# A 64-byte shift of the y buffers, a third seven-product piece in two blocks, and later loads of x and final_g, in a one-core gated short-convolution layer

## The chip, the cores and the metric

The kernel runs on one core of one Trainium2 chip. The metric is the device time of one execution in microseconds; the reported time is the median of several executions. One further execution is taken by the hardware profiler: the profile and its trace describe that execution.

## What is computed

`DEPTH` is 1, so the reference is one layer: an RMS norm of `x`, a modulation by `c` (adaLN), a gated short convolution, a gated residual, and a second RMS norm. D is 2048, E is 4096, the sequence has T = 256 tokens, all in float32.

```python
h = rmsnorm(x, norm_g)
mod = silu(c) @ ada_w + ada_b                  # shift, scale, gate: 3 x 2048
h = h * (1 + scale) + shift
b_gate, c_gate, v, g = split(h @ w_in, 4)      # w_in is 2048 x 16384
u = causal_depthwise_conv(c_gate * v, conv_w)  # width 3
y = b_gate * u * silu(g)                       # 256 x 4096
x = x + gate * (y @ w_out)                     # w_out is 4096 x 2048
return rmsnorm(x, final_g)
```

## The kernel before

**Precision.** Every large product is made of three products of a shorter float type: a float32 tile is split into `hi` (a rounding copy on ScalarE, `split_hi`, L315) and `lo` (the remainder, a subtraction on VectorE, `split_lo`, L320), and hi·hi, hi·lo and lo·hi are summed in PSUM.

**Input projection (L445).** The weights `w_in` are loaded tile by tile, split, and stand still in the array (`hi`, `lo`, 128x128 each); the tokens `hT` (hi and lo part of the modulated h, 16 tiles of 128 features) stream past, 256 columns per matmul. The first half of the columns is written to `mm_s` in an order planned by `plan()`, beside the sums that make shift and scale; the second half is written to `mm_b` by the loop over `ct` at L592. The results of a pair of 128 columns are gated, convolved and multiplied to y, and `split_y` (L396) stores hi and lo of y in a tile `ys[pair]`: 16 tiles of 128 x 2 x 2 x 256.

**Output projection (L753).** It runs over four blocks `dc` of 512 output columns. In a block, eight pieces `ep` of 512 rows of `w_out` are loaded by SyncE (`raw_o`, L771, 1 MB each), split, and multiplied with y. Here y stands still in the array and the split weights stream. A plain piece (`out_mm`, L640) has 2 token halves x 4 row tiles x 3 = 24 matmuls of 512 columns (L648, L649, L650). In the first three blocks the pieces in `SEVEN = (5, 6)` go another way (`seven`, L670): two 2x2 block products made with seven instead of eight block products (Winograd's form), 2 x 7 x 3 = 42 matmuls of 256 columns (L661). For these VectorE also forms sums of blocks of the weights (`sums_o`, L679, L685, L686), and the raw piece and the sums are each split (L684 and L687; L315 and L320). The matching sums of y are made once, in `token_forms` (L577, VectorE L583 to L586 and L590, ScalarE L589), into tiles `form`. `gather` (L715) adds the partial results at the end of a block on VectorE (L720), and `gated` (L791) multiplies by the gate, adds x, squares, and multiplies by `final_g` (L800 to L803). In the fourth block all eight pieces are plain, and each is first multiplied by the gate on VectorE (L778). The order of the pieces is `mix = (0, 1, 5, 2, 3, 6, 4, 7)`, in the fourth block 0 to 7.

**Buffers.** `hi`, the pieces loaded for the output projection and the splits each rotate over three buffers: tag `hi` holds the hi parts, tag `lo` holds `raw_o` and `sums_o`, tag `raw` holds the lo parts (and the first piece). A load waits until VectorE has read the tile that stood in its buffer. The stage's PSUM banks come in three pairs: one for `mm_o`, one for `mm_7`, one for the next block.

**Order.** A scheduler places each engine's instructions; SyncE issues nearly all loads in one queue, in order. x and `final_g` are loaded a second time for the end of the layer (L634, L635), into the tile `big`, which takes the space of `hT` and so waits for the last matmul of L445.

**Places in memory.** Pads named `line` to `line4` set where the buffers begin. In the built program the starts, counted in bytes past a multiple of 128 in each partition, are:

| buffer | used as | before | after |
|---|---|---|---|
| `hi`, `lo` in the input projection | stands still, L445 | 64 | 64 |
| `hT` | streams, L445 | 0 | 0 |
| `y`, `form` | stands still, L648 to L661 | 64 | 0 |
| `hi`, and `lo` in tag `raw` | streams, L648 to L661 | 64 | 64 |

All matmul operands begin at multiples of 256 bytes past these starts.

Of the kernel before, what the change touches and what calls it, by code (L numbers as in the profile page):

```python
# [31 lines left out]
ASLOT = 1024  # L32
# [85 lines left out]
def short_conv_layer(ctx: ExitStack, tc: tile.TileContext, x, c, norm_g, ada_w, ada_b, w_in, conv_w, w_out, final_g, out):  # L118
    nc = tc.nc
# [4 lines left out]
    line = ctx.enter_context(tc.tile_pool(name="line", bufs=1, side="right"))  # L124
    line.tile([P, 56], F32, tag="line", name="line")
    const = ctx.enter_context(tc.tile_pool(name="const", bufs=1))
    const.tile([P, 16], F32, tag="line0", name="line0")
    adap = ctx.enter_context(tc.tile_pool(name="adap", bufs=2))
    wpool = ctx.enter_context(tc.tile_pool(name="wpool", bufs=2))
    psum = ctx.enter_context(tc.tile_pool(name="psum", bufs=3, space=PSUM))  # L130
    hpool = ctx.enter_context(tc.tile_pool(name="hpool", bufs=1, side="right"))
    line2 = ctx.enter_context(tc.tile_pool(name="line2", bufs=1, side="right"))
    line2.tile([P, 48], F32, tag="line2", name="line2")
    slots = ctx.enter_context(tc.tile_pool(name="slots", bufs=NSLOT, side="right"))

    def slot(shape, name, dtype=F32):
# [157 lines left out]
    def modulate(k0, nk, sums):  # L294

        ks = slice(k0, k0 + nk)
        sums = sums.rearrange("p (s k) -> p s k", s=2)
        nc.vector.tensor_tensor(out=mod[:, :, ks], in0=sums, in1=bias[:, :, ks], op=ALU.add)
        for k in range(k0, k0 + nk):
            hf = xs[k // CT][:, k % CT, :]  # L300
            nc.scalar.activation(hh_[:, k], hf, AF.Identity, bias=mod[:, 0, k : k + 1], scale=mod[:, 1, k : k + 1])  # L301
# [3 lines left out]
            nc.vector.tensor_tensor(out=hl_[:, k], in0=hf, in1=hh_[:, k].bitcast(F32), op=ALU.subtract)  # L305

    def hi_tile():
        return wpool.tile([P, SLOT], F32R, tag="hi", name="hi", bufs=3)
# [132 lines left out]
    def product(dst, hi, lo, k, i, begins, left, ends):  # L441

        w, h = ((hi, hh_), (hi, hl_), (lo, hh_))[i]

        mm = last_mm[0] = nc.tensor.matmul(dst, w, h[:, k], start=begins and left, stop=ends, skip_group_check=True)  # L445
# [125 lines left out]

    KP = 8
    EP = 4
    SEVEN = (5, 6)
    forms = {}

    def token_forms(pair, u):  # L577

        sums = zs[0][:, 0].rearrange("p a (b f) -> p (a b) f", f=P)
        a11, a12 = u[:, 0, 0:P], u[:, 1, 0:P]  # L580
        a21, a22 = u[:, 0, P:T], u[:, 1, P:T]
        s1n, s2, s3, s4 = (sums[:, j] for j in range(4))
        nc.vector.scalar_tensor_tensor(out=s1n, in0=a21, scalar=-1.0, in1=a22, op0=ALU.mult, op1=ALU.subtract)  # L583
        nc.vector.scalar_tensor_tensor(out=s2, in0=s1n, scalar=-1.0, in1=a11, op0=ALU.mult, op1=ALU.subtract)
        nc.vector.tensor_tensor(out=s3, in0=a11, in1=a21, op=ALU.subtract)
        nc.vector.tensor_tensor(out=s4, in0=a12, in1=s2, op=ALU.subtract)  # L586
        form = adap.tile([P, ASLOT], F32R, tag="at", name="form", bufs=4)
        form = forms[pair] = form.rearrange("p (h s f) -> p h s f", h=2, f=P)
        nc.scalar.copy(form[:, 0], sums)  # L589
        nc.vector.tensor_tensor(out=form[:, 1], in0=sums, in1=form[:, 0].bitcast(F32), op=ALU.subtract)  # L590

    for ct in range(NS, NCT, 2):  # L592
        for q in QUARTERS:
# [34 lines left out]
        gate_piece()  # L628


    big = hpool.tile([P, 4, D], F32, tag="big", name="big")
    fg = big[:, 2, :]
    for t in range(TT):
        nc.sync.dma_start(big[:, t, :], x[t * P : (t + 1) * P, :])  # L634
    nc.sync.dma_start(fg, final_g.rearrange("(o d) -> o d", o=1).partition_broadcast(P))  # L635
    fsq = const.tile([P, TT, 4], F32, tag="fsq", name="fsq")
    LATE = 3
    NB = 256
# [31 lines left out]
    def seven(po, ps, ep, raw):  # L670
# [20 lines left out]
            return [ys[pair][:, k, h, t * P : (t + 1) * P] for h in range(2)]  # L691

        def f(pair, j):
            return [forms[pair][:, h, j] for h in range(2)]

        left, right = slice(0, NB), slice(NB, 2 * NB)
        for r in range(2):
# [17 lines left out]
    def gather(po, ps):  # L715


        res = big[:, 3, 0 : 2 * TT * NB].rearrange("p (t f) -> p t f", t=TT)
        u = big[:, 3, 2 * TT * NB :].rearrange("p (j f) -> p j f", f=NB)
        add = lambda out, a, b: nc.vector.tensor_tensor(out=out, in0=a, in1=b, op=ALU.add)  # L720
# [9 lines left out]
        return res  # L730

    part_sum = const.tile([P, TT], F32, tag="part_sum", name="part_sum")

# [14 lines left out]
            nc.sync.dma_start(out[t * P : (t + 1) * P, dd], r)  # L748

    n_ep = NCT // EP  # L750
    mix = (0, 1, 5, 2, 3, 6, 4, 7)
    orders = [mix, mix, mix, range(n_ep)]
    for dc in range(4):  # L753
        dcs = slice(dc * 512, (dc + 1) * 512)

# [11 lines left out]
        for ep in orders[dc]:  # L767

            first = dc == 0 and ep == 0
            raw = wpool.tile([P, SLOT], F32, tag="raw" if first else "lo", name="raw_o", bufs=3)  # L770
            nc.sync.dma_start(  # L771
                raw.rearrange("p (k f) -> p k f", k=EP),
                w_out[0, ep * EP * P : (ep + 1) * EP * P, dcs].rearrange("(k p) f -> p k f", p=P),
            )
            if dc == 3:

                raw3 = raw.rearrange("p (k f) -> p k f", k=EP)
                nc.vector.tensor_tensor(  # L778
                    out=raw3, in0=raw3, in1=gate(dc).unsqueeze(1).to_broadcast([P, EP, 512]), op=ALU.mult
                )  # L780
            if dc < 3 and ep in SEVEN:
                seven(po, ps, ep, raw)
                continue
            hi, lo = split(raw, SLOT, "raw")
            out_mm(po[0], 0, ep, hi, lo)
            if dc == 3 and ep >= n_ep - LATE:
                late.append((ep, hi, lo))
            else:
                out_mm(po[1], 1, ep, hi, lo)

        def gated(t, bank, c0, n):  # L791

            cs = slice(dc * 512 + c0, dc * 512 + c0 + n)
            r = big[:, t, cs]
            p0 = t * 512 + c0
            pr = big[:, 3, p0 : p0 + n]
            if dc == 3:
                nc.scalar.activation(pr, bank, AF.Square, scale=D**-0.5, accum_out=fsq[:, t, dc : dc + 1])
                return
# [7 lines left out]
                nc.vector.tensor_scalar_add(ps, ps, EPS)  # L807

        if dc < 3:
            res = gather(po, ps)  # L810
            po = [res[:, t] for t in range(TT)]
        gated(0, po[0], 0, 512)
        if dc == 3:
# [29 lines left out]
```

## Time and profile before

| what | value |
|---|---|
| median of 3 runs | 914.58 us (914.57 to 915.13) |
| the profiled execution | 915.32 us, of which 913.5 us are the span of its instructions |
| busy: PE, DVE, ACT | 894.8, 653.4, 476.4 us |
| first and last matmul of the output projection | start at 730.7 us and 903.5 us |
| matmuls of the output projection | 624 of 512 columns, 252 of 256 columns |

PE is TensorE's matmul row, DVE is VectorE, ACT is ScalarE, SPq is SyncE's queue. A row of a timeline begins with the start and the length in microseconds from the start of the span; `xN` joins N like instructions; in brackets stands the idle time of the engine before it and what ended it. A row of the groups ends with busy time, mean length in nanoseconds, and idle time before.

### The profile page before, as it was taken

How to read it: one execution, taken by the hardware profiler on the slowest of the kernel's cores; microseconds unless marked ns; L12 is line 12 of the kernel's file. 1: busy time of each engine (PE TensorE's matmuls, PEld its weight loads, DVE VectorE, ACT ScalarE, POOL GpSimd, SP SyncE). 2: the span in 40 equal slices, each digit the busy share in tenths (PEclk: the TensorE clock that was granted, in tenths of full speed). 3: DMA queues.
4: the chain of work that ended last, by engine and by line, in shares of the span. 5: the costliest groups of instructions: out<-in, count | busy, mean ns of one | idle time of the engine just before them, and what ended most of it. 6: DMA issues, size and time to landing. Idle time of an engine off the chain costs nothing.

```text
span 913.5 us, 16529 instructions
## 1 busy us (share of the span) xinstructions
PE 894.8 (98%) x7155; PEld 862.0 (94%) x7155; DVE 653.4 (72%) x655; ACT 476.4 (52%) x426; POOL 0.7 (0%) x6
## 2 busy tenths in 40 slices
PE   6999999999999999999999999999999999999995
PEld 4999999999999999999999999999999988888884
DVE  4889899989888886765545777555555567877992
ACT  6868856665558756743344434344433344444442
POOL 0000000000000000000000000000000000000000
PEclk9999999999999999999999999999999999999998
DMA  9999999999998686676666887556666476655642
GB/s 314 366 371 349 361 324 346 360 368 359 334 323 278 197 287 192 198 248 194 184 191 198 261 272 231 185 186 195 197 203 191 138 280 227 204 204 194 220 146 93
DMA packets 163753, 227.66 MB, mean 249 GB/s; under 512 B 5680, under 2 KB 104160, under 8 KB 163296
## 3 DMA queue, kind: packets, MB, share of 16 engines
q1 hardware_dynamic: 163552, 226.56, 75.0%
q8 instruction: 56, 0.92, 0.4%
q14 instruction: 17, 0.14, 0.0%
q10 hardware_dynamic: 128, 0.04, 0.0%
HBM read 224.49 MB, written 2.10 MB: 248 GB/s over the span
## 4 chain that ended last, share of the span: by engine, by line
PE 95%; DMA 3%; ACT 1%; DVE 0%; ACTq 0%; issue 0%; DVEq 0%
PE mm_s L445 38%; PE mm_b L445 38%; PE mm_o L649 4%; PE mm_o L650 4%; PE mm_o L648 4%; DMA raw_o<-in_sc_w_out_dram 2%; PE mm L661 2%; PE mm_o L661 1%; PE tp_idle L238 1%; DMA rows<-in_ada_b_dram 1%; PE mm_l L648 1%; PE mm_l L649 1%; PE mm_l L650 1%; PE sum L354 1%; ACT hi L315 0%; PE ps_gate L569 0%
## 5 line engine op out<-in xcount | busy, mean ns | idle before, releaser
L445 PE MATMUL mm_s<-hT,hi 128*128 128x256 f32 x2048 | 350.4, 277 | 0.1
L445 PE MATMUL mm_b<-hT,hi 128*128 128x256 f32 x2048 | 349.4, 276 | 0.0
L445 PEld LDWEIGHTS mm_s<-hT,hi 128*128 128x128 f32 x2048 | 308.2, 188 | 1.0 <-ACT hT L301 0.3
L445 PEld LDWEIGHTS mm_b<-hT,hi 128*128 128x128 f32 x2048 | 308.1, 188 | 0.5 <-issue 0.5
L445 PE MATMUL mm_b<-hT,lo 128*128 128x256 f32 x1024 | 282.6, 276 | 0.0
L445 PE MATMUL mm_s<-hT,lo 128*128 128x256 f32 x1024 | 282.2, 277 | 0.0
L320 DVE TENSOR_TENSOR lo<-raw,hi 128x2048 fp32r<-128x2048 f32 (+1 forms) x66 | 148.0, 2243 | 115.8 <-ACT hi L315 115.3
L315 ACT CAST hi<-raw 128x2048 fp32r<-128x2048 f32 (+1 forms) x66 | 123.7, 1874 | 195.1 <-PE mm_b L445 150.0
L445 PEld LDWEIGHTS mm_b<-hT,lo 128*128 128x128 f32 x1024 | 192.2, 188 | 0.5 <-issue 0.5
L445 PEld LDWEIGHTS mm_s<-hT,lo 128*128 128x128 f32 x1024 | 191.7, 188 | 0.3 <-DVE lo L320 0.2
L320 DVE TENSOR_TENSOR lo<-raw_s,hi 128x2048 fp32r<-128x2048 f32 (+1 forms) x80 | 147.5, 1849 | 36.6 <-ACT hi L315 35.6
L315 ACT CAST hi<-raw_s 128x2048 fp32r<-128x2048 f32 (+1 forms) x80 | 123.9, 1558 | 69.3 <-PE mm_s L445 58.9
L428 DVE SCALAR_TENSOR_TENSOR gv<-at,silu_c,gv 128x512 f32<-128x512 f32 x105 | 78.5, 749 | 2.5 <-DMA at<-in_ada_w_dram 0.8
L315 ACT CAST hi<-raw_o 128x2048 fp32r<-128x2048 f32 x26 | 49.6, 1907 | 58.1 <-DVE raw_o L778 24.0
L320 DVE TENSOR_TENSOR lo<-raw_o,hi 128x2048 fp32r<-128x2048 f32 x26 | 59.1, 2288 | 23.9 <-ACT hi L315 23.9
L466 ACT COPY acc<-mm_s 128x1024 f32<-128x1024 f32 x54 | 54.6, 1012 | 38.4 <-PE mm_s L445 38.4
L649 PE MATMUL mm_o<-lo,y 128*128 128x512 f32 x176 | 68.7, 390 | 0.8 <-DVE lo L320 0.8
L650 PE MATMUL mm_o<-hi,y 128*128 128x512 f32 x176 | 68.5, 389 | 0.0
L648 PE MATMUL mm_o<-hi,y 128*128 128x512 f32 x176 | 68.4, 390 | 0.0
L566 DVE SCALAR_TENSOR_TENSOR gacc<-at_g,silu_c,gacc 128x512 f32<-128x512 f32 x60 | 44.9, 748 | 6.2 <-DMA at_g<-in_ada_w_dram 5.2
L649 PEld LDWEIGHTS mm_o<-lo,y 128*128 128x128 f32 x176 | 33.1, 188 | 7.8 <-DVE lo L320 1.1
L650 PEld LDWEIGHTS mm_o<-hi,y 128*128 128x128 f32 x176 | 33.1, 188 | 6.7
(132 smaller groups left out, 584.4 us busy)
## 6 DMA issues: line engine op xcount, KB each, us to landing
raw<-in_sc_w_in_dram SPq DMA_DIRECT2D x64, 1024.0 KB, 5.6
raw_s<-in_sc_w_in_dram SPq DMA_DIRECT2D x47, 1024.0 KB, 7.5
raw_o<-in_sc_w_out_dram SPq DMA_DIRECT2D x32, 1024.0 KB, 5.2
at<-in_ada_w_dram SPq DMA_DIRECT2D x114, 256.0 KB, 7.8
raw_s<-in_sc_w_in_dram SPq DMA_DIRECT2D x33, 512.0 KB, 6.7
at_g<-in_ada_w_dram SPq DMA_DIRECT2D x32, 512.0 KB, 7.7
at<-in_ada_w_dram SPq DMA_DIRECT2D x6, 512.0 KB, 9.4
x<-in_x_dram SPq DMA_DIRECT2D x4, 512.0 KB, 6.1
```

The source lines that it names most:

```text
L238: nc.tensor.matmul(tp_idle, ident, ones[:, 0:1].to_broadcast([P, 512]), start=True, stop=True)
L315: nc.scalar.copy(hi[:, :n], raw[:, :n])
L320: nc.vector.tensor_tensor(out=lo[:, :n], in0=raw[:, :n], in1=hi[:, :n].bitcast(F32), op=ALU.subtract)
L354: nc.tensor.matmul(sums0[:, o * P : (o + 1) * P], rows[:, o // NK0, (o % NK0) * P : (o % NK0 + 1) * P], col.to_broadcast([P, P]), start=k ...
L428: nc.vector.scalar_tensor_tensor(out=gv, in0=at4[:, i], scalar=c_k, in1=gv, op0=ALU.mult, op1=ALU.add)
L445: mm = last_mm[0] = nc.tensor.matmul(dst, w, h[:, k], start=begins and left, stop=ends, skip_group_check=True)
L466: nc.scalar.copy(acc[ch, q], bank)
L566: nc.vector.scalar_tensor_tensor(out=ga, in0=at3[:, i, :], scalar=s, in1=ga, op0=ALU.mult, op1=ALU.add)
L648: nc.tensor.matmul(po, yh, hi[:, o], start=opens, stop=False, skip_group_check=True)
L649: nc.tensor.matmul(po, yh, lo[:, o], start=False, stop=False, skip_group_check=True)
L650: nc.tensor.matmul(po, yl, hi[:, o], start=False, stop=ct == NCT - 1, skip_group_check=True)
L661: mm = nc.tensor.matmul(dst, form[a], b, start=opens and i == 0 and bank not in first_of, stop=False, skip_group_check=True)
```

## The change

1. Pads: `line0` grows by 64 bytes, `line4` and `line2` shrink by 64 each. The tiles of `const`, `adap` (`form`, `at`, `gv`) and all slots (`y`, `z`, `gate`, `acc`, x) begin 64 bytes later; `hi`, `lo`, `raw` and `hT` stay.
2. `SEVEN` becomes `(5, 6, 7)`, used in the first two blocks; the third block keeps `(5, 6)`, the fourth stays plain. The sums of y for pairs 14 and 15 are made too. Their tiles find room in the two `gv` buffers and in a part `hT2` cut off from `hT` (its last two feature tiles, at the same address as before).
3. The order of the pieces becomes `(0, 1, 2, 5, 3, 6, 4, 7)`.
4. `big` has 3 rows of D, not 4; the scratch of `gather` and `gated` moves into the `z` tiles.
5. x and `final_g` are asked for inside the first block, behind the load of its fourth piece; in SyncE's queue of the built program they stand behind the fourth `raw_o` load of the block, where they stood behind the third.

```diff
-    const.tile([P, 16], F32, tag="line0", name="line0")
+    const.tile([P, 32], F32, tag="line0", name="line0")
...
-    line2.tile([P, 48], F32, tag="line2", name="line2")
+    line2.tile([P, 32], F32, tag="line2", name="line2")
...
-    wpool.tile([P, 32], F32, tag="line4", name="line4", bufs=1)
+    wpool.tile([P, 16], F32, tag="line4", name="line4", bufs=1)
...
-    hT = hpool.tile([P, KT, 2 * T], F32R, tag="big", name="hT")
-    hh_ = hT[:, :, 0:T]
-    hl_ = hT[:, :, T : 2 * T]
+    KB = KT - 2
+    hT = hpool.tile([P, KB, 2 * T], F32R, tag="big", name="hT")
+    hT2 = hpool.tile([P, KT - KB, 2 * T], F32R, tag="big2", name="hT2")
...
-    SEVEN = (5, 6)
+    SEVEN = (5, 6, 7)
...
-        form = adap.tile([P, ASLOT], F32R, tag="at", name="form", bufs=4)
-        form = forms[pair] = form.rearrange("p (h s f) -> p h s f", h=2, f=P)
-        nc.scalar.copy(form[:, 0], sums)
-        nc.vector.tensor_tensor(out=form[:, 1], in0=sums, in1=form[:, 0].bitcast(F32), op=ALU.subtract)
+        if pair < 14:
+            form = adap.tile([P, ASLOT], F32R, tag="at", name="form", bufs=4).rearrange("p (h s f) -> p h s f", h=2, f=P)
+            hi, lo = form[:, 0], form[:, 1]
+        elif pair == 14:
+            hi, lo = (adap.tile([P, 512], F32R, tag="gv", name="form_g").rearrange("p (s f) -> p s f", f=P) for _ in range(2))
+        else:
+            form = hpool.tile([P, 2, 4, P], F32R, tag="big2", name="form_h")
+            hi, lo = form[:, 0], form[:, 1]
+        forms[pair] = hi, lo
+        nc.scalar.copy(hi, sums)
+        nc.vector.tensor_tensor(out=lo, in0=sums, in1=hi.bitcast(F32), op=ALU.subtract)
...
-    big = hpool.tile([P, 4, D], F32, tag="big", name="big")
+    big = hpool.tile([P, 3, D], F32, tag="big", name="big")
+    res = zs[1].rearrange("p a b f -> p a (b f)")
     fg = big[:, 2, :]
-    for t in range(TT):
-        nc.sync.dma_start(big[:, t, :], x[t * P : (t + 1) * P, :])
-    nc.sync.dma_start(fg, final_g.rearrange("(o d) -> o d", o=1).partition_broadcast(P))
+
+    def load_ends(n):
+
+        if 0 <= n < TT:
+            nc.sync.dma_start(big[:, n, :], x[n * P : (n + 1) * P, :])
+        elif n == TT:
+            nc.sync.dma_start(fg, final_g.rearrange("(o d) -> o d", o=1).partition_broadcast(P))
...
-        res = big[:, 3, 0 : 2 * TT * NB].rearrange("p (t f) -> p t f", t=TT)
-        u = big[:, 3, 2 * TT * NB :].rearrange("p (j f) -> p j f", f=NB)
+        u = zs[0].rearrange("p a b f -> p (a b) f")
...
-    mix = (0, 1, 5, 2, 3, 6, 4, 7)
+    mix = (0, 1, 2, 5, 3, 6, 4, 7)
     orders = [mix, mix, mix, range(n_ep)]
+    sevens = [SEVEN, SEVEN, SEVEN[:2], ()]
...
-            if dc < 3 and ep in SEVEN:
+            if dc == 0:
+                load_ends(orders[dc].index(ep) - 3)
+            if ep in sevens[dc]:
                 seven(po, ps, ep, raw)
                 continue
```

More of the change, by code (lines that the diff above doesn't have):

```diff
@@ L269, in short_conv_layer, with tokens @@
     nc.vector.reciprocal(rstd, rstd)
-    hT = hpool.tile([P, KT, 2 * T], F32R, tag="big", name="hT")
-    hh_ = hT[:, :, 0:T]
-    hl_ = hT[:, :, T : 2 * T]
+    KB = KT - 2
+    hT = hpool.tile([P, KB, 2 * T], F32R, tag="big", name="hT")
+    hT2 = hpool.tile([P, KT - KB, 2 * T], F32R, tag="big2", name="hT2")
+    def tokens(k, part):
+        return (hT[:, k] if k < KB else hT2[:, k - KB])[:, part * T : (part + 1) * T]
+    hh_ = [tokens(k, 0) for k in range(KT)]
+    hl_ = [tokens(k, 1) for k in range(KT)]
     xs = [slot([P, CT, T], f"xs{j}") for j in range(KT // CT)]
@@ L300, in modulate @@
             hf = xs[k // CT][:, k % CT, :]
-            nc.scalar.activation(hh_[:, k], hf, AF.Identity, bias=mod[:, 0, k : k + 1], scale=mod[:, 1, k : k + 1])
+            nc.scalar.activation(hh_[k], hf, AF.Identity, bias=mod[:, 0, k : k + 1], scale=mod[:, 1, k : k + 1])
             nc.vector.tensor_scalar(
@@ L304, in modulate @@
             )
-            nc.vector.tensor_tensor(out=hl_[:, k], in0=hf, in1=hh_[:, k].bitcast(F32), op=ALU.subtract)
+            nc.vector.tensor_tensor(out=hl_[k], in0=hf, in1=hh_[k].bitcast(F32), op=ALU.subtract)
     def hi_tile():
@@ L443, in product @@
         w, h = ((hi, hh_), (hi, hl_), (lo, hh_))[i]
-        mm = last_mm[0] = nc.tensor.matmul(dst, w, h[:, k], start=begins and left, stop=ends, skip_group_check=True)
+        mm = last_mm[0] = nc.tensor.matmul(dst, w, h[k], start=begins and left, stop=ends, skip_group_check=True)
         if begins and left:
@@ L693, in f @@
         def f(pair, j):
-            return [forms[pair][:, h, j] for h in range(2)]
+            return [forms[pair][h][:, j] for h in range(2)]
         left, right = slice(0, NB), slice(NB, 2 * NB)
@@ L729, in gather @@
         add(res[:, 1], po[1], u[:, 0:2].rearrange("p j f -> p (j f)"))
-        return res
     part_sum = const.tile([P, TT], F32, tag="part_sum", name="part_sum")
@@ L794, in gated @@
             r = big[:, t, cs]
-            p0 = t * 512 + c0
-            pr = big[:, 3, p0 : p0 + n]
+            pr = res[:, t, c0 : c0 + n]
             if dc == 3:
@@ L809, in short_conv_layer @@
         if dc < 3:
-            res = gather(po, ps)
+            gather(po, ps)
             po = [res[:, t] for t in range(TT)]
```

## Prediction

> **What bounds the kernel now.** I read the page first: busy time, the slices, the chain that ended last.
>
> ```profile
> PE 894.8 (98%) x7155; PEld 862.0 (94%) x7155; DVE 653.4 (72%) x655; ACT 476.4 (52%) x426; POOL 0.7 (0%) x6
> ...
> PE   6999999999999999999999999999999999999995
> ...
> DVE  4889899989888886765545777555555567877992
> ...
> PEclk9999999999999999999999999999999999999998
> ...
> PE 95%; DMA 3%; ACT 1%; DVE 0%; ACTq 0%; issue 0%; DVEq 0%
> ```
>
> TensorE is busy from the second slice to the last but one, at a full granted clock, and 95% of the chain is TensorE. So time is won where TensorE gets fewer or quicker matmuls, and lost where another engine is late for it. VectorE is the only other one near its limit (9 tenths at the end). The waits of TensorE after 700 us come next; there is only one row:
>
> ```profile
> PE mm_o L649 <- DVE lo L320: 0.8, 1, 0.8
> ```
>
> The change touches the output projection, so I ask what one matmul costs there and in the input projection. A busy row overlaps its neighbours; what counts is the distance from start to start. First a stretch of the chain (start, length), then TensorE's timeline of one plain piece and one seven-product piece.
>
> ```profile
> 380.98 160.93 PE mm_b L445 x1420
> ```
> ```profile
> 779.84 0.39 PE L650 MATMUL mm_o<-hi,y 128*128 128x512 f32 x1
> ...
> 785.28 0.39 PE L650 MATMUL mm_o<-hi,y 128*128 128x512 f32 x1
> 785.50 0.28 PE L661 MATMUL mm<-hi,y 128*128 128x256 f32 x1
> ...
> 790.54 0.40 PE L648 MATMUL mm_o<-hi,y 128*128 128x512 f32 x1
> ```
>
> L445, 256 columns: 160.93 / 1420 = 113.3 ns each. L661, 256 columns: 42 matmuls from 785.50 to 790.54, 120.0 ns each. L648 to L650, 512 columns: 24 from 779.84 to 785.28, 226.7 ns each. So the same width, with the same 128x128 weights, costs 6.7 ns more in the output projection; and if a column costs the same in both widths there (226.7 - 120.0 = 106.7 for 256 columns), each matmul carries 6.7 ns beside its columns in L445 and 13.3 ns in L648 to L661. What differs is in the table of starts: in L445 the operand that stands still begins 64 bytes past a multiple of 128 and the one that streams at 0, 64 apart; in the output projection both begin at 64, 0 apart. After the change they are 64 apart again (0 and 64).
>
> **The shift and the third piece: TensorE.** By the code the output projection has 18 + 8 = 26 plain pieces x 24 = 624 matmuls of 512 columns and 6 x 42 = 252 of 256 columns. At the measured distances: 624 x 0.2267 + 252 x 0.120 = 141.5 + 30.2 = 171.7 us. After: 24 plain pieces, 576 matmuls, and 8 seven-product pieces, 336 matmuls. I take for all 912 the 6.7 ns less that L445 shows: 576 x 0.2200 + 336 x 0.1133 = 126.7 + 38.1 = 164.8 us. That is **-6.9 us**, of which the third piece alone is 2 x (5.44 - 5.04) = 0.8 at the old distances, and the shift about 6.1. No row shows the new pairing itself, so I bound it: no gain from the shift, 576 x 0.2267 + 336 x 0.120 = 170.9 us, -0.8; and as far to the other side, 177.0 us, +5.3. I take the gain, as L445 has the same distance of 64 and 6144 matmuls.
>
> The shift also moves buffers that only VectorE, ScalarE and DMAs use; L445's own operands keep their places, and the transposes shift both operands alike. No row shows those at another start, and I take nothing: in the slices of the input projection's second half VectorE is idle four tenths of the time, so slower instructions would be covered there; in the output projection they would lengthen the chain computed below.
>
> **The later loads.** Queue of SyncE, then ScalarE, then the page's row of loads:
>
> ```profile
> 730.94 0.82 SPq L634 DMA_DIRECT2D big<-in_x_dram  x2
> 731.80 0.43 SPq L635 DMA_DIRECT2D big<-in_final_g_dram  x1
> 732.33 64.41 SPq L771 DMA_DIRECT2D raw_o<-in_sc_w_out_dram  x13
> ```
> ```profile
> 743.60 1.90 ACT L315 CAST hi<-raw_o 128x2048 fp32r<-128x2048 f32 x1 [4.62 <-DMA raw_o<-in_sc_w_out_dram]
> ```
> ```profile
> raw_o<-in_sc_w_out_dram SPq DMA_DIRECT2D x32, 1024.0 KB, 5.2
> ```
>
> x and final_g, 3 MB, go out at 730.94 to 731.80, when the last L445 matmul frees `hT`. The block's fourth piece, asked for at 732.33, is behind them and reaches ScalarE at 743.60, 11.3 us later instead of 5.2; its split ends too late and makes the 0.8 us wait. After, pieces 0, 1, 2 and 5 are asked for ahead of x, so the first late one is the fifth. It arrives no later than about 747 (one more megabyte ahead of it, some 3 us at the pace of the rows); with 1.9 for hi and 2.3 for lo it is ready at 751. TensorE wants it at 730.7 + 3 x 5.28 + 4.76 = 751.3. The wait goes: **-0.8 us**; if the cover fails it comes back as about as much. One ScalarE copy of x into PSUM (L766) waits for x a little longer with hi casts behind it; those are wanted after 748, about ten microseconds later. The x and final_g rows are first read by `gated` at the end of block one.
>
> **The sums of y for two more pairs.**
>
> ```profile
> L590 DVE TENSOR_TENSOR form<-z,form 128x512 fp32r<-128x512 f32 x4 | 2.7, 684 | 0.0
> ...
> L586 DVE TENSOR_TENSOR z<-z,z 128x128 f32<-128x128 f32 x4 | 1.2, 292 | 0.1
> L583 DVE SCALAR_TENSOR_TENSOR z<-z 128x128 f32<-128x128 f32 x4 | 1.2, 292 | 0.1
> L584 DVE SCALAR_TENSOR_TENSOR z<-z,z 128x128 f32<-128x128 f32 x4 | 1.1, 284 | 0.0
> L585 DVE TENSOR_TENSOR z<-z 128x128 f32<-128x128 f32 x4 | 1.1, 283 | 0.0
> ```
> ```profile
> L589 ACT CAST form<-z 128x512 fp32r<-128x512 f32 x4 | 2.5, 614 | 0.0
> ```
> ```profile
> 400.00:735.00 335.00, 335.00 (x2928) 333.32 (x2927) 193.46 (x166) 136.31 (x104) 0.00 (x0) 1.00 0.65 204
> ```
>
> Per pair 0.68 + 4 x 0.29 = 1.8 us of VectorE and 0.6 of ScalarE. Between 400 and 735 us VectorE works 193 of 335 and TensorE never stops, so pair 14 costs nothing. Pair 15 comes at the start of the first block, in front of piece 2's lo, which has 10.6 us of pieces 0 and 1 before it. Cost nothing; uncovered 1.8.
>
> **VectorE in the output projection.** Here I expect something to be given back. Its timeline around a seven-product piece, and the groups of the block's end:
>
> ```profile
> 830.46 4.50 DVE L320 TENSOR_TENSOR lo<-raw_o,hi 128x2048 fp32r<-128x2048 f32 x2 [1.93 <-ACT hi L315]
> 834.87 1.22 DVE L679 TENSOR_TENSOR sums_o<-raw_o 128x1024 f32<-128x1024 f32 x1
> 836.01 1.75 DVE L687 TENSOR_TENSOR lo<-raw_o,hi 128x1536 fp32r<-128x1536 f32 x1
> 837.68 0.68 DVE L685 TENSOR_TENSOR sums_o<-raw_o,sums_o 128x512 f32<-128x512 f32 x1
> 838.40 0.69 DVE L686 TENSOR_TENSOR sums_o<-raw_o,sums_o 128x512 f32<-128x512 f32 x1
> 841.13 2.29 DVE L320 TENSOR_TENSOR lo<-sums_o,hi 128x2048 fp32r<-128x2048 f32 x1 [2.04 <-ACT hi L315]
> ...
> 851.08 2.29 DVE L778 TENSOR_TENSOR raw_o<-raw_o,gate 128x2048 f32<-128x2048 f32 x1
> ```
> ```profile
> L800 DVE TENSOR_TENSOR big<-big,gate 128x512 f32<-128x512 f32 x6 | 4.0, 681 | 0.0
> L803 DVE TENSOR_TENSOR big<-big 128x512 f32<-128x512 f32 x6 | 3.9, 684 | 0.0
> L801 DVE TENSOR_TENSOR big<-big 128x512 f32<-128x512 f32 x6 | 3.9, 681 | 0.0
> ...
> L720 DVE TENSOR_TENSOR big<-mm_o,big 128x256 f32<-128x256 f32 x6 | 2.2, 412 | 0.0
> L720 DVE TENSOR_TENSOR big<-mm,big 128x512 f32<-128x512 f32 x3 | 2.1, 685 | 0.0
> L720 DVE TENSOR_TENSOR big<-mm_o,big 128x512 f32<-128x512 f32 x3 | 2.0, 678 | 0.0
> ...
> L720 DVE TENSOR_TENSOR big<-mm,big 128x256 f32<-128x256 f32 x3 | 1.3, 417 | 0.0
> L720 DVE TENSOR_TENSOR big<-big,mm 128x256 f32<-128x256 f32 x3 | 1.2, 415 | 0.0
> ```
>
> The four operations of a seven-product piece take 834.87 to 839.09, 4.22 us. Then VectorE waits 2.04 for ScalarE's hi of the sums and makes their lo; a lo costs 2.21 from start to start (two end after 4.50). One such piece and the plain one behind it therefore occupy VectorE's queue for 4.22 + 2.04 + 2.21 + 2.21 = 10.7 us, waits included. TensorE consumes the two in 5.04 + 5.44 = 10.5 now and 4.76 + 5.28 = 10.0 after. Before, two plain pieces lie between the two seven-product ones, so VectorE has 15.9 us of TensorE's time for 12.9 of its own. After, the order 5, 3, 6, 4, 7 leaves one: five such steps (two in each of the first two blocks, one in the third), each 0.64 short, 3.2 us. Across a block's end the queue holds, from one seven-product piece to the next, 2.04 + 4 x 2.21 + 8.8 / 3 of gather + 2.6 of gating and adding + 4.22 = 20.6, against TensorE's 3 x 5.28 + 4.76 = 20.6: no lead is won back there. Bounds: 0 if a lead outlives the steps, 3.2 if none does. I take **+3.0**, since the gather now comes wholly after the last piece of the block and uses the lead up.
>
> In the fourth block VectorE has 8 x 4.4 us (a gate product L778 and a lo) plus 6.9 of the third block's end; TensorE's 8 x 5.28 = 42.2 is as long, and VectorE's lead at its start is that of before. Nothing.
>
> **Sum.** -6.9 - 0.8 + 3.0 = -4.7 us. The profiled execution took 915.32 (span 913.5 and 1.8 around it), so it would take 910.6; the median of the runs is 0.74 below it, and 914.58 - 4.7 = **909.9 us**.
>
> **The rivals.** *The shift does nothing* (it doesn't do what it says). L445 and L661 also differ in what streams: `hT` starts at 0 and the weights at 64 past 128, and the latter does not change. If the streaming operand's own start costs the 6.7 ns, 170.9 us remain: -0.8 for the third piece, -0.8 for the wait, and 0 to 1.0 for five steps that are 0.2 short (10.7 against 10.5): 913.0 to 914.0. For it: no row has a still operand at 0. Against it: nothing says which of the two starts matters, and only the pair tells L445 and L661 apart as well. The Trainium skill speaks for this rival: "TensorE: Matmul & The Clock Gate", in "Step-by-step: what each phase is for", gives TensorE two independent read ports, so that loading the next weights takes nothing from the running matmul. By that page the place of y against the stream could not matter, and the sum would be this rival's 913.0; whether it holds here no row of this trace decides.
>
> *The chain of VectorE costs more.* A load may land late: the raw piece of the next seven-product piece goes into the buffer that L686 frees, so load and four operations take 5.2 + 4.22 = 9.4 of the 10.7; a load of 6.9 would be 11.1, 0.4 more per step, and the two block ends could lose some 0.5 each. That is up to 3 us more: 910 to 913.
>
> *Slower: the new pairing is worse.* If a still operand at a multiple of 128 bytes costs another 6.7 ns per matmul, the stage takes 177.0 us: +5.3 - 0.8 = +4.5, 919.1; VectorE's steps are then covered. It decides from 3.8 ns per matmul on (912 x 3.8 ns = 3.5 us, which eats 1.6 of gains and adds 0.2%). Against it: L445, 64 apart.
>
> **How the numbers follow.** Forecast, with waits from 0 to 3.2: 0.70. The shift does nothing: 0.15. A dearer chain: 0.07. Slower: 0.08. The low end is the forecast without waits, 914.58 - 6.9 - 0.8 = 906.9; the high end takes in the dearer chain and half of the rival without effect, 913.5. About 0.2% (1.8 us) is what a measurement of this kernel can tell from no change. Faster by more: 0.70 + 0.07 = 0.77; within: 0.15; slower: 0.08.
>
> **What would show it.** L661 at 113.3 ns and L648 at 220 from start to start: the shift works; 120 and 226.7: it does not. No wait for a lo of `raw_o` near 747: the loads. TensorE's waits for `lo<-sums_o` of about 0.3 to 0.6 us in the second and third seven-product piece of a block: VectorE's chain. I am wrong if the distances do not move, if TensorE's waits sum to more than 5 us, or if L445 leaves 113.3 ns.

## The result, and the profile after

The changed kernel takes **916.01 us** (median of 22 runs, 915.09 to 917.07), the kernel before beside it on the same chips 914.59 (22 runs, 913.89 to 915.33). The ratio is 1.0016, with a 95% interval of 1.0010 to 1.0023: it is 1.4 us slower. That is within the 0.2% (1.8 us) that the prediction counted as no change, the interval reaching just past it, and on the slow side, where the forecast was 909.9. The profiled execution took 916.7 us, its span 914.6 at a granted clock of 0.997, as before.

The page of the kernel after, the lines that answer to those of before (busy time, slices, the chain that ended last):

```profile
PE 897.3 (98%) x7191; PEld 862.6 (94%) x7191; DVE 665.3 (73%) x673; ACT 480.6 (53%) x430; POOL 0.7 (0%) x6
...
PE   6999999999999999999999999999999999999996
...
DVE  4889899989888886765545776555555567888992
...
PEclk9999999999999999999999999999999999999998
...
PE 97%; ACT 1%; DMA 1%; ACTq 0%; issue 0%; DVE 0%
```

TensorE bounds the kernel as it did. It is now 97% of the chain, against 95, and the view of its matmuls' waits after 700 us has no row left: the 0.8 us for `lo` is gone. Its weight loads (PEld) still have three rows, 0.8 us together:

```profile
PEld mm L680 <- DVE lo L326: 0.3, 2, 0.2
PEld mm L680 <- ACT hi L703: 0.3, 1, 0.3
PEld mm_o L667 <- ACT hi L321: 0.2, 1, 0.2
```

VectorE has 12 us more work (665.3 against 653.4), and two of its slices near the end are a tenth busier. Nothing in these lines says why the time rose: the weight loads' waits were 1.1 us before, so the waits by themselves speak for a gain. Only the distances from start to start tell otherwise.

First the input projection, a stretch of the chain (start, length), then TensorE's timeline of the output projection (start, length): three plain pieces, with a seven-product piece behind them.

```profile
381.10 160.93 PE mm_b L451 x1420
```

```profile
774.33 0.39 PE L668 MATMUL mm_o<-lo,y 128*128 128x512 f32 x1
...
790.88 0.28 PE L680 MATMUL mm<-hi,y 128*128 128x256 f32 x1
...
795.83 0.39 PE L667 MATMUL mm_o<-hi,y 128*128 128x512 f32 x1
```

L451 keeps its 113.3 ns. From 774.33 to 790.88 there are 71 matmuls of 512 columns, **233.1 ns** each, where L648 to L650 took 226.7. From 790.88 to 795.83 there are 42 of 256 columns, **117.9 ns** each, where L661 took 120.0. So the shift moved both widths, in opposite directions, and the wider one the wrong way.

The whole stage, from the start of its first matmul to that of its last, took 172.73 us before and 174.38 after, 1.65 more (the mean distances here and below are those of neighbouring starts, with the few long ones, where TensorE waits, counted apart). The sum closes:

| term | before | after | us |
|---|---|---|---|
| 576 matmuls of 512 columns | 227.07 ns | 233.24 ns | +3.55 |
| 336 matmuls of 256 columns | 119.78 ns | 116.64 ns | -1.06 |
| third piece: 48 of 512 for 84 of 256 columns, at the distances of before | 10.90 us | 10.06 us | -0.84 |
| long distances, beyond a normal one | 1.08 us near 747 | 1.1 us in ten small ones, 760 to 847 | 0 |

The span rose by less, 1.1: the stage began 0.15 later, and what follows its last matmul took 0.7 less, which was not pursued.

The long distances are two things that cancel. The one near 747 is gone. TensorE's timeline, then ScalarE's:

```profile
744.89 0.40 PE L667 MATMUL mm_o<-hi,y 128*128 128x512 f32 x1
...
747.23 0.40 PE L668 MATMUL mm_o<-lo,y 128*128 128x512 f32 x1
```
```profile
747.93 1.91 ACT L321 CAST hi<-raw_o 128x2048 fp32r<-128x2048 f32 x1 [3.69 <-PE mm_o L669]
```

Ten matmuls in 2.34 us, 234 ns each, without a hole; and the first cast whose load now goes out behind x, that of the block's fifth piece, waits for a buffer that TensorE frees and not for its load. In its place come ten small ones of 0.05 to 0.17 us. VectorE's timeline, from one seven-product piece to the next, shows where the first two are from:

```profile
752.08 1.22 DVE L698 TENSOR_TENSOR sums_o<-raw_o 128x1024 f32<-128x1024 f32 x1
753.22 1.75 DVE L706 TENSOR_TENSOR lo<-raw_o,hi 128x1536 fp32r<-128x1536 f32 x1
754.88 0.69 DVE L704 TENSOR_TENSOR sums_o<-raw_o,sums_o 128x512 f32<-128x512 f32 x1
755.61 0.69 DVE L705 TENSOR_TENSOR sums_o<-raw_o,sums_o 128x512 f32<-128x512 f32 x1
758.35 2.29 DVE L326 TENSOR_TENSOR lo<-sums_o,hi 128x2048 fp32r<-128x2048 f32 x1 [2.05 <-ACT hi L321]
760.56 2.28 DVE L326 TENSOR_TENSOR lo<-raw_o,hi 128x2048 fp32r<-128x2048 f32 x1
762.76 1.22 DVE L698 TENSOR_TENSOR sums_o<-raw_o 128x1024 f32<-128x1024 f32 x1
```

The chain of the prediction is there, 752.08 to 762.76, 10.68 us for its 10.7. The `lo` of the sums ends at 760.64, just when TensorE's timeline has one of its small holes (its rows stand below, with the experiment on the two streams). The two largest of the third block, 0.24 us from 838.76, end otherwise. TensorE waits there for ScalarE's hi of the raw piece (L703), and this cast for its load:

```profile
837.60 1.48 ACT L703 CAST hi<-raw_o 128x1536 fp32r<-128x1536 f32 x1 [1.63 <-DMA raw_o<-in_sc_w_out_dram]
```

The load is asked for at 831.38, just behind the end of VectorE's last sum of the seven-product piece before (L705, 831.31), which frees a buffer. So VectorE's chain is at the root there too, but by way of a late load, which the prediction had as a rival ("The chain of VectorE costs more").

### The profile page after: what moved, and what is told of

It reads as the page before. It is cut to its first block, busy times and chain, and to the rows that moved or that the text cites. A ratio compares the mean times of both kernels' runs of the same rounds, so it can differ in the third digit from the quotient of the medians.

```text
span 914.6 us, 16626 instructions
## 1 busy us (share of the span) xinstructions
PE 897.3 (98%) x7191; PEld 862.6 (94%) x7191; DVE 665.3 (73%) x673; ACT 480.6 (53%) x430; POOL 0.7 (0%) x6
## 4 chain that ended last, share of the span: by engine, by line
PE 97%; ACT 1%; DMA 1%; ACTq 0%; issue 0%; DVE 0%
PE mm_b L451 38%; PE mm_s L451 38%; PE mm_o L667 4%; PE mm_o L669 4%; PE mm_o L668 4%; PE mm L680 3%; PE mm_o L680 2%; PE tp_idle L238 1%; PE mm_l L667 1%; DMA rows<-in_ada_b_dram 1%; PE mm_l L668 1%; PE mm_l L669 1%; PE sum L360 1%; PE ps_gate L575 0%; PE tp_g L441 0%; PE tp_x L290 0%
## 5 line engine op out<-in xcount | busy, mean ns | idle before, releaser
L451 PE MATMUL mm_s<-hT,hi 128*128 128x256 f32 x2048 | 350.4, 277 | 0.1
L451 PE MATMUL mm_b<-hT,hi 128*128 128x256 f32 x2048 | 349.4, 276 | 0.0
L451 PEld LDWEIGHTS mm_s<-hT,hi 128*128 128x128 f32 x2048 | 308.5, 188 | 1.0 <-ACT hT L307 0.3
L451 PEld LDWEIGHTS mm_b<-hT,hi 128*128 128x128 f32 x2048 | 308.4, 188 | 0.5 <-issue 0.5
L451 PE MATMUL mm_b<-hT,lo 128*128 128x256 f32 x1024 | 282.6, 276 | 0.0
L451 PE MATMUL mm_s<-hT,lo 128*128 128x256 f32 x1024 | 282.2, 277 | 0.0
L451 PEld LDWEIGHTS mm_b<-hT,lo 128*128 128x128 f32 x1024 | 192.2, 188 | 0.5 <-issue 0.5
L451 PEld LDWEIGHTS mm_s<-hT,lo 128*128 128x128 f32 x1024 | 191.8, 188 | 0.3
L321 ACT CAST hi<-raw_o 128x2048 fp32r<-128x2048 f32 x24 | 45.8, 1909 | 48.8 <-DVE raw_o L796 23.9
L326 DVE TENSOR_TENSOR lo<-raw_o,hi 128x2048 fp32r<-128x2048 f32 x24 | 54.9, 2290 | 12.5 <-ACT hi L321 12.2
L667 PE MATMUL mm_o<-hi,y 128*128 128x512 f32 x160 | 63.4, 396 | 0.0
L669 PE MATMUL mm_o<-hi,y 128*128 128x512 f32 x160 | 63.3, 395 | 0.0
L668 PE MATMUL mm_o<-lo,y 128*128 128x512 f32 x160 | 63.3, 395 | 0.0
L484 ACT COPY mm_s<-acc 128x1024 f32<-128x1024 f32 x38 | 38.5, 1017 | 0.7
L668 PEld LDWEIGHTS mm_o<-lo,y 128*128 128x128 f32 x160 | 30.1, 188 | 7.0
```

The source lines that it names most:

```text
L321: nc.scalar.copy(hi[:, :n], raw[:, :n])
L326: nc.vector.tensor_tensor(out=lo[:, :n], in0=raw[:, :n], in1=hi[:, :n].bitcast(F32), op=ALU.subtract)
L451: mm = last_mm[0] = nc.tensor.matmul(dst, w, h[k], start=begins and left, stop=ends, skip_group_check=True)
L484: nc.scalar.copy(bank, acc[ch, q])
L667: nc.tensor.matmul(po, yh, hi[:, o], start=opens, stop=False, skip_group_check=True)
L668: nc.tensor.matmul(po, yh, lo[:, o], start=False, stop=False, skip_group_check=True)
```

## The experiments

The theory that I test first, S: the shift costs time in matmuls of 512 columns. Its rival, D: the time is lost to VectorE's longer chain and the moved loads, and would be lost without the shift too. Each ratio is against the kernel before, run beside it on the same chip; the profile of one execution gives the stage in microseconds and the mean distances at 512 and at 256 columns, in this order.

### The change without the shift, and the shift alone

```
# after, without the shift (e1)            # before, with the shift alone (e2)
line0: [P, 32] -> [P, 16]                  line0: [P, 16] -> [P, 32]
line2: [P, 32] -> [P, 48]                  line2: [P, 48] -> [P, 32]
line4: [P, 16] -> [P, 32]                  line4: [P, 32] -> [P, 16]
```

> The changed kernel with the pads, and so the starts of all buffers, as before. Theory S (the shift of y costs time in the 512-column matmuls): their distance goes back to 227 ns and that of the 256-column ones to 120; with the third seven-product piece (-0.8 us) and the later loads (-0.8 us) the time is 1.0 to 1.6 us under that of the kernel before. Rival D (the extra VectorE work and the moved loads cost it): the time stays at that of the changed kernel, 1.4 us over the one before.

> The kernel before with the pads of the changed one. Theory S: 624 matmuls of 512 columns at 233 ns instead of 227 and 252 of 256 columns at 117 instead of 120, +3.9 - 0.8 = about +3 us. Rival D: no change.

Without the shift: 913.82 us against 914.45, ratio 0.9992 (0.9983 to 1.0001), stage 171.67, 227.41 and 119.16 ns. The shift alone: 917.13 against 914.45, ratio 1.0032 (1.0020 to 1.0043), stage 175.39, 233.28 and 115.65 ns. TensorE's timeline of the shift alone, four plain pieces up to a seven-product one:

```profile
763.08 0.39 PE L648 MATMUL mm_o<-hi,y 128*128 128x512 f32 x1
...
785.47 0.28 PE L661 MATMUL mm<-hi,y 128*128 128x256 f32 x1
```

96 matmuls in 22.39 us, 233.2 ns, with the loads and the work of VectorE as before. So S holds and D falls: the pads alone add 2.7 us, and all else in the change together is worth -0.6 by the medians, whose interval just reaches no change, and -1.06 by the stage. The medians' 0.6 is less than the 1.0 to 1.6 us expected: 0.87 us of small waits came back.

### Every distance by itself

The two widths, each with eight starts of the still and eight of the streaming operand, in steps of 32 bytes; nothing else runs beside it.

```
for wide in (512, 256):
    for i in range(8):
        for j in range(8):
            ...
            yh, yl = (still[:, 8 * i + 256 * h : 8 * i + 256 * h + P] for h in range(2))
            hi, lo = (stream[:, 8 * j + 1024 * h : 8 * j + 1024 * h + wide] for h in range(2))
            terms = [(yh, hi), (yh, lo), (yl, hi)] * 10
```

> Leaves out the layer: only matmuls in the pattern of the output projection (yh hi, yh lo, yl hi), 30 for each of 8 starts of the still operand x 8 starts of the streaming operand, in steps of 32 bytes over 256, once with 512 and once with 256 columns. Theory P (the distance of the two starts within 128 bytes sets the time of a matmul): one value for each distance, the same for both widths, with 227 or 120 ns at distance 0. Rival A (the still operand's own start): one value for each row of still starts, worse at multiples of 128. Rival H (the time depends on how the two pipelines stand to each other when a stretch begins, not on the starts alone): values that differ between sections with the same distance.

TensorE's timeline (start, length; p is 512 and q 256 columns, then the start of the still and that of the streaming operand in steps of 32 bytes from a; the distance between two starts, by 30, is one matmul):

```profile
20.27 6.96 PE L39 MATMUL paa<-stream,still 128*128 128x512 f32 x30
27.07 7.16 PE L39 MATMUL pab<-stream,still 128*128 128x512 f32 x30
34.07 7.03 PE L39 MATMUL pac<-stream,still 128*128 128x512 f32 x30
40.94 7.17 PE L39 MATMUL pad<-stream,still 128*128 128x512 f32 x30
...
61.97 7.17 PE L39 MATMUL pag<-stream,still 128*128 128x512 f32 x30
68.97 7.16 PE L39 MATMUL pah<-stream,still 128*128 128x512 f32 x30
75.97 7.16 PE L39 MATMUL pba<-stream,still 128*128 128x512 f32 x30
82.97 6.99 PE L39 MATMUL pbb<-stream,still 128*128 128x512 f32 x30
89.79 7.16 PE L39 MATMUL pbc<-stream,still 128*128 128x512 f32 x30
...
465.95 3.75 PE L39 MATMUL qaa<-stream,still 128*128 128x256 f32 x30
469.54 3.70 PE L39 MATMUL qab<-stream,still 128*128 128x256 f32 x30
...
487.29 3.60 PE L39 MATMUL qag<-stream,still 128*128 128x256 f32 x30
490.72 3.71 PE L39 MATMUL qah<-stream,still 128*128 128x256 f32 x30
```

512 columns: `paa` 6.80 / 30 = 226.7 ns, `pab` 233.3, `pac` 229.0, `pag` 233.3. With both operands 32 bytes further `pbb` is 227.3 again, and `pba` 233.3. What counts is **the start of the streaming operand less that of the still one, modulo 256 bytes**, and the width. So P was wrong in two points, the modulus (it had 128) and one value for both widths, and A falls: at 512 columns the still operand's own start makes no difference, only the distance does. 256 columns: `qaa` 119.7, `qag` 114.3 (113.3 once the first six distances within it are over). For a still operand at its first start, the mean between neighbours within a section past the first six:

| stream - still, bytes modulo 256 | 0 | 32 | 64 | 96 | 128 | 160 | 192 | 224 |
|---|---|---|---|---|---|---|---|---|
| 512 columns, ns | 226.7 | 233.3 | 228.8 | 233.4 | 233.5 | 234.3 | 233.3 | 233.3 |
| 256 columns, ns | 120.0 | 117.8 | 117.7 | 120.0 | 118.8 | 117.4 | 113.3 | 118.4 |

All eight diagonals for 512 columns repeat within about 1 ns. For 256 columns the 192 has two values: five of its eight sections ran at 113.7 to 114.7, three at 117.7. So there, as H had it, sections with one distance differ.

Put back into the kernel: `hT` at 0 against `hi` at 64 is 192, 256 wide: 113.3, as L445 and L451 run (their `lo`, for a third of the matmuls, stands at 192, a distance of 64, and the mixture keeps 113.3). Before, the output projection is at 0: 226.7 and 120.0, as L648 to L661 ran. After, 64 less 128 is 192 again: 233.3 and 113.3 to 117.7, as L667 to L680 run (but for the `form` of pair 15, 24 of the 336, which stands at 0, a distance of 64). The starts of y in the built program are 64 before and 128 after, modulo 256; the table of starts ahead of the prediction gives them modulo 128, which hides the sign.

### The shift for the forms alone

By the grid, the streams of the seven-product pieces should gain against `form`, which can move by itself, while y stays at a distance of 0.

```
# after, with y back (line0 and line4 as after)
line2: [P, 32] -> [P, 48]
```

> The changed kernel with y back at its old start and only the sums of y (form) shifted: streams start 0 past y's start and 192 past that of form, modulo 256 (64 for pair 15). Theory G (the grid: the time of a matmul goes by the streaming start minus the still start modulo 256, and by the width: 512 columns 226.7 ns at 0 and 233.3 at 192; 256 columns 120.0 at 0 and 113.3 to 118 at 192): 512-column matmuls at 227, the 24 form matmuls of a seven-product piece quicker than 120, so 0.4 to 1.2 us under the unshifted version of the changed kernel, less what VectorE's chain gives back. Rival A (a still operand at a multiple of 128 bytes is what costs): the form matmuls get slower than 120 and the time is 1 us over the unshifted version.

913.60 us against 914.46, ratio 0.9993 (0.9984 to 1.0001), stage 171.67, 227.38 and 117.9 ns. The 512 columns are back, and the 256 columns take 1.3 ns less than without any shift, 336 x 1.3 = 0.4 us. The small waits take it back: 1.31 us of long distances against 0.87 without the shift. The stage is the same 171.67, and the 0.4 to 1.2 us expected did not come: the quicker TensorE seems only to have met VectorE sooner.

### The later loads alone

```
# the change without the shift, and without the third piece
SEVEN = (5, 6, 7) -> (5, 6)
```

> The changed kernel without the shift and without the third seven-product piece: only the order (0, 1, 2, 5, 3, 6, 4, 7), the later loads and the z tiles as scratch are left. Theory L (the later loads take away the 0.8 us wait of the first block): 0.8 us under the kernel before, with waits of at most 0.6 us for VectorE in the steps 5, 3, 6. Rival N (they only move the wait): no change, with a wait of about 0.8 us at another place of the first block.

914.09 us against 914.46, ratio 0.9999 (0.9990 to 1.0008): the medians don't separate it from nothing. The profile does: the distances of 1.20 and 0.34 us near 747 are gone, 0.32 us of others come, and the stage is 171.96 against 172.73, 0.77 less.

### The two streams apart

Does each matmul have its own price by its own distance, so that a triple's mean is the sum of three? The grid again, the still operand at 0, `hi` at one start and `lo` at another.

```
yh, yl = still[:, 0:P], still[:, 256 : 256 + P]
hi, lo = stream[:, 8 * i : 8 * i + wide], stream[:, 1024 + 8 * j : 1024 + 8 * j + wide]
```

> Leaves out the layer: the pattern yh hi, yh lo, yl hi again, with the still operand at one start and the starts of hi and lo moved apart, 8 x 8 steps of 32 bytes, for 512 and for 256 columns. Theory G1 (each matmul's time goes by its own streaming start against its own still start): the value is the mean of two times the hi distance and once the lo distance of the first grid. Rival G2 (it goes by the streaming start of one matmul against the still start of the next, whose load runs beside it): the same mean here, as all still starts are alike; but if stretches lock, a row is not additive and has values outside those of the first grid.

It doesn't. At 512 columns (again past the first six) 226.7 is found only with both at a distance of 0; all others are 228.8 to 235.4. At 256 columns there is 116.7 to 121.3 and no section at 113.3, not even the one whose operands stand where `qag` had them, both streams at 192:

```profile
657.17 3.70 PE L39 MATMUL qgg<-stream,still 128*128 128x256 f32 x30
660.71 3.73 PE L39 MATMUL qgh<-stream,still 128*128 128x256 f32 x30
```

3.54 / 30 = 118.0 ns with the same operands for which the other grid shows 114.3. So a stretch can keep one of two paces, and between these two sections only what came ahead of them differs. In the run of the shift alone, all six seven-product pieces stand at 192 and none has a long distance within it: three ran at 113.5 or 113.6 ns, three at 117.8. The kernel after changes its pace within one piece; TensorE's timeline around the wait for the `lo` of the sums:

```profile
758.35 0.28 PE L680 MATMUL mm_o<-hi,y 128*128 128x256 f32 x1
...
760.47 0.28 PE L680 MATMUL mm_o<-hi,y 128*128 128x256 f32 x1
760.70 0.38 PE L680 MATMUL mm<-lo,form 128*128 128x256 f32 x1
760.92 0.39 PE L680 MATMUL mm<-hi,form 128*128 128x256 f32 x2
...
763.30 0.39 PE L667 MATMUL mm_o<-hi,y 128*128 128x512 f32 x1
```

18 matmuls from 758.35 to 760.47, 117.8 ns each; two distances that are 0.11 longer, about when VectorE's `lo` ends at 760.64; then 21 from 760.92 to 763.30, 113.3 each.

### The sums ahead of the raw piece's lo

Now the small waits. Theory C: they are VectorE's chain. In it `lo` of the raw piece (L706, 1.75 us) goes ahead of the last two sums, so that ScalarE's hi of the sums, and with it their `lo`, starts late. Rival: they are ScalarE's or a load's, and stay.

```
# on the kernel with the shift for the forms alone
s4 = nc.vector.tensor_tensor(out=s[:, :, 3], in0=b[:, :, 3], in1=s[:, :, 2], op=ALU.subtract)
rest = nc.vector.tensor_tensor(out=bl[:, :, 1:4], in0=b[:, :, 1:4], in1=..., op=ALU.subtract)
tc.add_manual_dep(rest.ins, s4.ins.name, after, reason="sums first")
...
orders = [mix, mix, (0, 1, 5, 2, 3, 6, 4, 7), range(n_ep)]
```

> The version with only form shifted, with the four VectorE operations of a seven-product piece in the order sums first, lo of the raw piece last (so that ScalarE's hi of the sums runs beside it), and the third block's pieces in the old order (two plain pieces between the seven-product ones). Theory C (VectorE's chain of 10.7 us for a seven-product and a plain piece makes TensorE's small waits): the chain is about 1.8 us shorter, the long distances in the 256-column stretches go away, and the time falls by about 1.3 us, their sum in the form-shifted version. Rival R (the long distances come from TensorE's own restart or from loads): they stay.

912.89 us against 914.80, ratio 0.9979 (0.9970 to 0.9988); stage 170.33, 1.34 less than without this edit, and no long distance is left. VectorE's timeline, the same place:

```profile
750.73 1.22 DVE L698 TENSOR_TENSOR sums_o<-raw_o 128x1024 f32<-128x1024 f32 x1
751.99 0.69 DVE L704 TENSOR_TENSOR sums_o<-raw_o,sums_o 128x512 f32<-128x512 f32 x1
752.71 0.69 DVE L705 TENSOR_TENSOR sums_o<-raw_o,sums_o 128x512 f32<-128x512 f32 x1
753.32 1.75 DVE L706 TENSOR_TENSOR lo<-raw_o,hi 128x1536 fp32r<-128x1536 f32 x1
755.45 2.29 DVE L326 TENSOR_TENSOR lo<-sums_o,hi 128x2048 fp32r<-128x2048 f32 x1 [0.38 <-ACT hi L321]
759.13 2.29 DVE L326 TENSOR_TENSOR lo<-raw_o,hi 128x2048 fp32r<-128x2048 f32 x1 [1.38 <-ACT hi L321]
```

L706 now lies where VectorE stood waiting for ScalarE: the wait in front of the sums' `lo` is 0.38 instead of 2.05, the `lo` ends 7.0 us after the first sum instead of 8.6, and VectorE even has to wait for the plain piece's hi behind it. C holds for the first two blocks, where only the dependence was changed and all the long distances, 0.65 of the 1.31 us, went. In the third block, where the other 0.66 stood, from TensorE's wait for a cast whose load came late, the order of the pieces was changed too, and which of the two edits removed it was not tried.

### The raw piece 64 bytes lower

The grid as a tool: for y at 64 the raw piece of a seven-product piece should begin at 0, a distance of 192.

```
# on top of the edit before
bh, bl = (v...[:, :, NB - 16 : 4 * NB - 16]... for v in (hi, lo))
nc.scalar.copy(bh, b[:, :, 1:4])
```

> The version before this one, with hi and lo of the raw part of a seven-product piece written 64 bytes further down in their tiles (their first quarter is unused), so that 12 of its 18 matmuls stream 192 past the start of y instead of 0, and 6 stream 128 past form instead of 192. Theory G (the grid): these 18 take 113 to 119 ns instead of 118 to 120, so 0.3 to 0.8 us less in all. Rival H (in a mixed stretch a matmul's time goes by how the stretch began): no change.

**911.68 us** against 914.80, ratio 0.9967 (0.9954 to 0.9979); stage 169.93, 0.4 less, 227.05 and 117.2 ns. TensorE's timeline, a seven-product piece and three plain ones:

```profile
767.09 0.28 PE L680 MATMUL mm<-hi,y 128*128 128x256 f32 x1
...
771.97 0.40 PE L667 MATMUL mm_o<-hi,y 128*128 128x512 f32 x1
...
788.32 0.28 PE L680 MATMUL mm<-hi,y 128*128 128x256 f32 x1
```

42 in 4.88 us, 116.2 ns each; 72 in 16.35, 227.1. This version is quicker than both kernels. The stage explains 0.4 of the 1.2 us between the medians of this and the edit before; the profiled execution of that one lies at the low end of its runs (912.05 of 912.03 to 913.40), and where its other runs spend more no trace here shows.

### A rival for the reason: the still operand at a multiple of 128

The grid forecasts for y at 0 modulo 256 (one pad fewer; the streams at 64 as before, the forms unmoved) a distance of 64: 228.8 ns at 512 columns. Rival A, from the prediction: a still operand at a multiple of 128 bytes costs 6.7 ns whatever streams, so 233.3.

```
# before, without these lines
line2 = ctx.enter_context(tc.tile_pool(name="line2", bufs=1, side="right"))
line2.tile([P, 48], F32, tag="line2", name="line2")
```

> The kernel before with y alone moved 192 bytes up, to a multiple of 256, form where it was. The weights stream 64 past y modulo 256. Theory G (the grid): 512-column matmuls 228.8 ns instead of 226.7, +1.3 us; the 18 y matmuls of a seven-product piece about 118 instead of 120, -0.3: about +1 us. Rival A (a still operand at a multiple of 128 bytes costs 6.7 ns per 512-column matmul): 233 ns as in the changed kernel, about +3.5 us.

914.98 us against 914.80, ratio 1.0003 (0.9994 to 1.0012); stage 173.32, 228.92 and 117.65 ns. TensorE's timeline, 42 matmuls:

```profile
774.77 0.39 PE L647 MATMUL mm_o<-lo,y 128*128 128x512 f32 x1
...
784.38 0.39 PE L647 MATMUL mm_o<-lo,y 128*128 128x512 f32 x1
```

9.61 / 42 = 228.8 ns, the grid's number. A falls here too. The stage's +0.59 is 623 x 1.85 - 252 x 2.13 ns = 0.61 us; the medians can't tell it from no change.

## Why the prediction was wrong

**The step that failed** is the shift's term in "The shift and the third piece: TensorE": "I take the gain, as L445 has the same distance of 64 and 6144 matmuls." Sign, width and modulus were lost in it. L445 (its `hi`) and the output projection after the change do have one distance, 192 modulo 256, but L445 streams 256 columns, and 512 columns behave otherwise: at 192 they take 6.6 ns more than at 0, not 6.7 less. That is +3.55 us where 576 x 6.7 ns = 3.9 us of gain was forecast, a miss of 7.4. With the misses below (+1.2 for the 256 columns, -1.9 for VectorE's waits and -0.3 for the wait near 747) this makes 6.4, what lies between the forecast of -4.7 and the stage's +1.65; by the medians it is 6.1. The premise before it, "if a column costs the same in both widths there", carried 256-column evidence over to 512 columns; the grid shows the order of the distances turned round between the widths (512: best at 0; 256: 0 among the worst).

**The 256 columns** had the right sign and half the size: 3.1 ns less, -1.06 us, where 336 x 6.7 ns = 2.2 us was forecast. A stretch keeps 117.8 or 113.3, and more of them kept the slower one (the mean is 116.64).

**The third piece alone**, -0.8: right for its matmuls, 0.84 at the old distances. The run without the shift and the run with the later loads alone differ by nothing else. Their stages are 171.67 and 171.96, so only 0.29 was left of it: long distances rose from 0.32 to 0.87 us.

**The later loads**, -0.8: right (1.08 with the second, shorter hole). The wait near 747 is gone in the kernel after and with the loads alone, where the stage is 0.77 shorter.

**The sums of y for two more pairs**, nothing: right. Those of pair 15 are done at 736.4, and TensorE has no long distance before 760.

**VectorE in the output projection**, +3.0: the mechanism was right, its size not. The chain took 10.68 us, and in the first two blocks its waits went when the sums were put first. But each step is the chain less TensorE's time for two pieces, and TensorE didn't get quicker: at the distances of after these two take 42 x 117.9 + 24 x 233.2 ns = 10.55 us, not 10.0. So a step was short by 0.1, not 0.64, and all waits came to 1.1 us, those of the third block's late load among them. The prediction's own rival without effect had 0 to 1.0 for that.

**The rivals.** "The new pairing is worse" was the right one in mechanism: its price of 6.7 ns for a matmul of 512 columns is close to what was measured, 6.2 in the kernel and 6.6 in the grid. Its reason, a still operand at a multiple of 128 bytes, fell with the grid and with y at 0. It charged 912 matmuls where 576 paid, so it gave 919.1, which is 3.1 too much. "The shift does nothing" fell: 913.82 is what the kernel takes without it, in the 913 to 914 that this rival gave. The rule that spoke for it stands in the Trainium skill, "TensorE: Matmul & The Clock Gate", section "Step-by-step: what each phase is for": two independent read ports keep the next weights' load from taking read bandwidth from the running matmul. What the prediction drew from it, that the place of y against the stream could not matter, does not hold here: with nothing else running, 512 columns take 226.7 to 234.3 ns by the distance of the two operands. Whether the load does take bandwidth no run here shows.

**The chances.** 0.77 for faster rested on one pair of rows (L445 against L661) that differed in which operand was at which start, and the text said that "no row shows the new pairing itself" and bounded it at +5.3. Between bounds of -6.9 and +5.3 with one analogue of another width, the chance should have been nearer even, and the range should have reached past 914. The signs of being wrong named distances that do not move, not ones that move the wrong way.

**What stays open.** Why the distance matters as it does, why 512 and 256 columns differ, and what sets one of two paces at 192. The grids show the dependence, not its cause; that the reads of the two operands meet in the memory is a guess that no run here tests.

## What to carry to other kernels

A pace found for one shape says nothing of another: before moving a buffer, ask for a row with the same width and the same signed distance, modulo 256 bytes, of the two operands, and if there is none, measure the grid first (one kernel, 0.7 ms). A gain on the bounding engine brings the next engine's chain into view, so look for an order in which that chain uses its own waits: here putting 1.4 us of sums ahead of 1.75 us of other work, with the third block's old order of pieces, gave 1.3 us of the stage. And a view of the matmuls' waits with no rows doesn't mean that nothing was lost: compare distances from start to start.

## What the runs showed of the hardware that was not expected

A matmul with its own 128x128 weights takes 226.7 to 234.3 ns at 512 and 113.3 to 120.0 ns at 256 columns, by the start of the stream less that of the still operand modulo 256 bytes: 3 and 6%, at a granted clock of 1.0 with nothing else running. The best distance is 0 for 512 and 192 for 256 columns. With two streams at different distances the paces don't add (at 512 columns 226.7 only with both at 0). And one arrangement of 256 columns can run at 117.8 or at 113.3: the same operands took 114.3 in one grid and 118.0 in the other, and in the kernel after a piece changed from 117.8 to 113.3 behind two holes of 0.11 us.
